# A planner inside the kernel sets the order on every engine; cache splits move to ACT and GpSimd

## The chip, the cores and the metric

The kernel runs on one core of a Trainium2 chip. A core has five engines with a queue each, worked off in order: PE (TensorE, matmuls), DVE (VectorE), ACT (ScalarE), POOL (GpSimd) and SP, which here only issues DMAs. Matmuls write PSUM, which DVE and ACT read; POOL works between SBUF tiles. The metric is the time of one execution on the device in microseconds (us); lower is better. Times are medians of a few runs, and one more execution is taken with the hardware profiler.

## The reference

The reference is one step of a two-layer hybrid encoder. It has 512 new prompt frames (called P below: four tiles of 128 rows) and 8 running streams with 16 new frames each (called S: one tile of 128 rows), and the streams have 1024 cached positions per layer.

```python
def trunk_layer(x, q_pos, past, ...):
    p = x @ w_in
    a_u, a_v, b_cq, b_ckv, b_kr, c_q, c_k, c_v = jnp.split(p, in_split_points(), axis=-1)
    y_a = spatial_gate(u, layer_norm(gelu(a_v)), w_s, b_s)
    # latent attention: scores against cached and new ckv and krope, softmax, values are ckv
    out_lat = sweep_query_blocks(lambda qp, ql, qr: mla_attend(qp, ql, qr, ckv_all, kr_all, k_pos),
                                 q_pos, q_lat, q_rope)
    # stick-breaking attention: log-sigmoid, suffix sum, exp, cached and new k and v
    y_c = sweep_query_blocks(lambda qp, qq: sb_attend(qp, qq, k_all, v_all, k_pos), q_pos, qc)
    y = jnp.concatenate([rms_norm(y_a, g_a), rms_norm(y_b, g_b), rms_norm(y_c, g_c)], -1)
    x = layer_norm(ALPHA * x + y @ w_out, ln1_g, ln1_b)
    h = jnp.square(jax.nn.relu(x @ w_up + b_up)) @ w_down + b_down
    return layer_norm(ALPHA * x + h, ln2_g, ln2_b), (ckv, krope, kc, vc, v)
```

Each layer runs for P (no past) and for S (with the cache). All numbers are float32.

## The kernel before

**Split products.** Each float32 operand is split into a high half, a rounding cast to fp32r (on ACT, `act.copy`), and a low half, the difference (`sub`, on DVE unless another engine is named). `mm3` then does three fp32r matmuls: high by high, high by low, low by high. So every weight tile and cache tile that is loaded costs a cast, a subtraction and its matmuls.

**Work per layer.** P projects all five row tiles at once (`in`, `mix`), and beside it does its stick-breaking attention and the gate. Then come P's latent attention (`lane_pmla`: tiles ckT, knT, krT, vM, qT, pT), its output projection, and the MLP in groups of four 128-wide slices (`w_up` in tile wx, `w_down` in tile w or w8, activations in hT). S is a second thread: `s_prep`, latent attention over the cache (`lane_smla`), stick-breaking attention over the cache (`lane_ssb`), output projection and MLP (tile wS). S takes its rows from P's projection of the same layer, and P's next layer takes S's row tile.

**The cache pieces of S.** Keys come as 128 x 512 pieces: DMA to rawK, ACT cast to cT, DVE subtraction to cT (`sample_scores`, L1106). In the latent attention every second key piece has a rope piece too, krs to kr, with the cast on ACT and the subtraction of the lower 64 partitions on DVE (L1201). Values come as 128 x 512 pieces: DMA to rawV, DVE cast to cN, POOL subtraction to cN (`sample_values`, L1143, L1144). Each of these tags has two buffers.

**What sets the order.** `weave` and `lanes` interleave the generators of P and S by a rough running clock for each engine (`Pace`, `cost_of`) and by shares of PE time (`RATE`). The program thus written then goes to the framework's own scheduler, which orders each engine's queue by its own estimates. The framework adds all waits on semaphores and the reuse of buffers; the order on an engine is fixed when the program is built. Nearly all instructions carry line L109, that of the recording helper, so groups go by tile names. In the trace, w8 reads w.

Of the kernel before, what the change touches and what calls it, by code (L numbers as in the profile page):

```python
# [44 lines left out]
FW = 3.0  # L45

# [5 lines left out]
class Pace:  # L52


    def __init__(self):
        self.free = dict(pe=0.0, act=0.0, dve=0.0, pool=0.0)
        self.done, self.read, self.slots = {}, {}, {}
        self.pe = self.t = 0.0

    def add(self, key, cost, out, ins):  # L60
        s = max([self.free[key]] + [self.done.get(x, 0.0) for x in (out, *ins)])
        self.t = self.free[key] = s + cost
        self.done[out] = self.t + 0.1
        for x in ins:
            self.read[x] = self.t + 0.1
# [17 lines left out]
def cost_of(key, name, out, ins):  # L83
    n = math.prod(out.shape[1:])
    if name == "transpose":
        return 0.109 if ins[0].dtype == F32 else 0.056
    if key == "pe":
        return max(n / 2400, math.prod(ins[0].shape[1:]) / 1200)
    if name in ("tensor_reduce", "bn_stats"):
        n = math.prod(ins[0].shape[1:])  # L90
    return {"act": 0.11 + n * 0.00072, "dve": 0.07 + n * (0.00052 if name == "tensor_copy" else 0.00104),
            "pool": 0.07 + n * 0.0023}[key]


class Timed:
# [5 lines left out]
    def __getattr__(self, name):  # L101
        f = getattr(self.eng, name)
        if name.startswith("preload"):
            return f

        def call(out, *a, **k):
            ins = [x for x in (*a, *k.values()) if isinstance(x, bass.AP)]
            self.pace.add(self.key, cost_of(self.key, name, out, ins), out.tensor.name, [x.tensor.name for x in ins])
            return f(out, *a, **k)  # L109
        return call  # L110

# [48 lines left out]
def hybrid_step(  # L160
# [9 lines left out]
    ld, pace = nc.sync, Pace()  # L170
# [4 lines left out]
    cp = ecx(tc.tile_pool(name="const", bufs=1))  # L175
    rawp = ecx(tc.tile_pool(name="raw", bufs=1))
    wp = ecx(tc.tile_pool(name="w8", bufs=4))
    xp = ecx(tc.tile_pool(name="xy", bufs=1))
    sm = ecx(tc.tile_pool(name="small", bufs=3))
    drp = ecx(tc.tile_pool(name="scr", bufs=1, space=DRAM))  # L180
    ps = ecx(tc.tile_pool(name="ps", bufs=1, space=PSUM))
# [11 lines left out]

    act.preload_act_table_set("natural_log_exp_and_others")
# [1338 lines left out]
```

## Time and profile before

| | us |
|---|---|
| median of 3 runs | 1856.31 (1853.24 to 1859.94) |
| the profiled execution | 1860.24 |
| its span, first to last instruction | 1858.5 |
| PE busy in the span | 1724.9 |
| DVE busy | 1307.1 |
| ACT busy | 931.0 |
| POOL busy | 342.6 |

Busy is the time in which an engine has at least one instruction running. A matmul's end is modelled and overlaps the next one's start, so PE's busy time is more than its work. [...] In the profile's rows, "out<-in" names the tile written and the tiles read, and what stands behind "<-" at the end of a row is what the instruction waited for.

### The profile page before, as it was taken

Reading aid. Unit: us, or ns where it says so; the run is one execution under the profiler, and the core shown is the slowest. Engines: PE = TensorE matmul, PEld = TensorE weight load, DVE = VectorE, ACT = ScalarE, POOL = GpSimd, SP = SyncE. Lnnn points to the kernel's source line nnn. Section 1 sums busy time; section 2 is a strip of 40 time slices with the busy share of each in tenths; the row PEclk is TensorE's granted clock in tenths of the full one; section 3 lists DMA queues with packets and bytes.
Section 4 is the critical chain, followed back from the end, with each engine's and each line's share of the span. In section 5 each row is a group of like instructions: output and inputs, shape, how many; then the busy total and the mean of one; then the engine's idle time right before and its main releaser. Section 6 shows DMA issues by size and latency. Waiting matters only on the chain. (4 is left out here: it accounts for less than half of the span.)

```text
span 1858.5 us, 24372 instructions
## 1 busy us (share of the span) xinstructions
PE 1724.9 (93%) x8756; PEld 1460.2 (79%) x8756; DVE 1307.1 (70%) x1870; ACT 931.0 (50%) x1613; POOL 342.6 (18%) x338
## 2 busy tenths in 40 slices
PE   8998897989999999999799988979899999999997
PEld 7887785878778888888688876858787778888886
DVE  3576978687885577676626768886878765776766
ACT  4674756245653346564227547661455623465641
POOL 0023123350213110001000321323502332000001
PEclk9998979989999999999899988889999999999999
DMA  7225654544544467784442245554445433776852
GB/s 260 89 79 156 185 180 143 177 128 141 183 136 130 135 243 253 215 265 149 133 157 83 75 155 179 182 164 147 140 136 170 147 113 104 259 240 215 268 162 90
DMA packets 145817, 305.05 MB, mean 164 GB/s; under 512 B 32032, under 2 KB 46496, under 8 KB 145696
## 3 DMA queue, kind: packets, MB, share of 16 engines
q1 hardware_dynamic: 145696, 303.49, 51.1%
q8 instruction: 69, 1.13, 0.3%
q14 instruction: 52, 0.43, 0.1%
HBM read 286.14 MB, written 17.30 MB: 163 GB/s over the span
## 5 line engine op out<-in xcount | busy, mean ns | idle before, releaser
L109 PE MATMUL acc<-w,hT 128*128 128x512 f32 x1536 | 399.5, 401 | 6.7 <-DVE xy L109 3.9
L109 PE MATMUL acc<-yT,wx 128*128 128x512 f32 (+1 forms) x1632 | 397.0, 388 | 6.7 <-ACT wx L109 3.2
L109 PEld LDWEIGHTS acc<-yT,wx 128*128 128x128 f32 x1632 | 298.4, 194 | 68.1 <-ACT wx L109 3.7
L109 PEld LDWEIGHTS acc<-w,hT 128*128 128x128 f32 x1536 | 288.7, 191 | 75.0 <-DVE xy L109 6.4
L109 POOL TENSOR_TENSOR cN<-rawV,cN 128x512 fp32r<-128x512 f32 x128 | 196.2, 1538 | 605.9 <-DVE cN L109 584.8
L109 DVE TENSOR_TENSOR w<-rawP,w 128x1024 fp32r<-128x1024 f32 (+4 forms) x122 | 147.9, 1213 | 135.7 <-ACT w L109 134.5
L109 DVE TENSOR_TENSOR wS<-rawS,wS 128x1024 fp32r<-128x1024 f32 x144 | 175.6, 1223 | 84.8 <-ACT wS L109 84.1
L109 ACT CAST wS<-rawS 128x1024 fp32r<-128x1024 f32 x144 | 151.0, 1052 | 128.3 <-PE sC L109 50.4
L109 ACT CAST w<-rawP 128x1024 fp32r<-128x1024 f32 (+4 forms) x122 | 122.4, 1006 | 179.4 <-DMA rawP<-in_w_down_dram 105.7
L109 PE MATMUL acc<-w,xT 128*128 128x512 f32 (+3 forms) x960 | 194.3, 355 | 0.0
L109 PEld LDWEIGHTS acc<-w,xT 128*128 128x128 f32 x960 | 161.8, 197 | 15.5 <-DVE ev L109 0.4
L109 DVE TENSOR_TENSOR xy<-xy,acc 128x512 f32<-128x512 f32 x128 | 85.8, 682 | 49.1 <-PE acc L109 48.4
L109 POOL TENSOR_SCALAR rs<-mv 128x1 f32<-128x1 f32 x20 | 14.2, 710 | 518.9 <-DVE mv L109 518.4
L109 ACT CAST cT<-rawK 128x512 fp32r<-128x512 f32 x128 | 78.7, 620 | 54.9 <-DMA rawK<-in_t_sbk_dram 17.8
L109 PE MATMUL x<-wS,htS 128*128 128x512 f32 x384 | 105.3, 394 | 0.0
L109 DVE TENSOR_TENSOR cT<-rawK,cT 128x512 fp32r<-128x512 f32 x128 | 93.7, 738 | 16.2 <-ACT cT L109 15.5
L109 PE MATMUL sC<-wS,x1TS 128*128 128x512 f32 x384 | 103.4, 393 | 0.0
L109 PE MATMUL x<-cN,pTs 128*128 128x256 f32 x512 | 91.1, 293 | 11.6 <-POOL cN L109 7.1
L109 PEld LDWEIGHTS x<-cN,pTs 128*128 128x128 f32 x512 | 78.9, 195 | 23.0 <-POOL cN L109 9.4
L109 DVE TENSOR_TENSOR wx<-rawP,wx 128x1024 fp32r<-128x1024 f32 x68 | 85.5, 1262 | 11.3 <-ACT wx L109 10.9
L109 DVE CAST cN<-rawV 128x512 fp32r<-128x512 f32 x128 | 73.2, 578 | 27.7 <-PE x L109 14.9
L109 PEld LDWEIGHTS sC<-wS,x1TS 128*128 128x128 f32 x384 | 72.0, 188 | 16.4
(278 smaller groups left out, 2808.1 us busy)
## 6 DMA issues: line engine op xcount, KB each, us to landing
rawP<-in_t_wup_dram SPq DMA_DIRECT2D x64, 512.0 KB, 4.0
rawP<-in_w_down_dram SPq DMA_DIRECT2D x64, 512.0 KB, 4.3
rawS<-in_w_up_dram SPq DMA_DIRECT2D x64, 512.0 KB, 4.5
rawS<-in_w_down_dram SPq DMA_DIRECT2D x64, 512.0 KB, 4.4
rawK<-in_t_ckv_dram SPq DMA_DIRECT2D x64, 256.0 KB, 3.2
rawV<-in_t_ckvv_dram SPq DMA_DIRECT2D x64, 256.0 KB, 3.0
rawK<-in_t_sbk_dram SPq DMA_DIRECT2D x64, 256.0 KB, 3.2
rawV<-in_t_sbv_dram SPq DMA_DIRECT2D x64, 256.0 KB, 2.9
```

The costliest lines, as they stand in the source:

```text
L109: return f(out, *a, **k)
```

## The change

Three parts. First, every instruction and DMA is noted when it is written (`Plan.note`), with its engine, a duration from a formula per engine and operation (`cost_of`), and its dependencies. Second, at the end a list schedule over the whole program is made (`Plan.schedule`): each engine, and SP for DMAs, takes at its next free moment the instruction with the lowest rank of those that are ready, and buffers and pools are granted in turn. The rank is the progress of a thread in its layer: P by its PE time, S by its time on other engines, with S laid between 0.25 and 0.93 of P's layer. `Plan.follow` then ties each engine's instructions to that order. Third, three kinds of work change engine: the cast of cached values goes from DVE to ACT (the subtraction stays on POOL), the subtractions of cached keys and of rope keys go from DVE to POOL. The matmuls are the same.

```diff
+SPAN = 0.25, 0.93
...
+class Plan:
+    AFTER = dict(pe=0.17, act=0.0, dve=0.0, pool=0.0, sp=0.0)
+    HOP = dict(pe=0.055, act=0.035, dve=0.035, pool=0.08, sp=0.03)
+    LAP = dict(pe=0.0, act=0.1, dve=0.08, pool=0.0, sp=0.0)
...
+    def ranks(self, lo, hi):
+        total, at = collections.Counter(), []
+        for o in self.ops:
+            key = o["by"], int(o["phase"][-1])
+            total[key] += o["cost"] if (o["eng"] == "pe") == (o["by"] == "P") and o["eng"] != "sp" else 0.0
+            at.append((key, total[key]))
+        at = [(c / max(total[k], 1e-9), k) for k, c in at]
+        at = [(k[1] + (f if k[0] == "P" else lo + (hi - lo) * f), i) for i, (f, k) in enumerate(at)]
...
+        def issue(k, e, s):
+            nonlocal dma
+            o = ops[k]
+            if o["kind"] == "copy":
+                s = max(s, free["pool"])
+            if e == "sp":
+                free[e] = s + 0.42
+                dma = max(dma, s + 1.3) + o["bytes"] / 320e3
+                f = dma + 0.45
+            else:
+                free[e] = s + o["cost"] - self.LAP[e]
+                f = s + o["cost"] + self.AFTER[e]
+                if o["kind"] == "copy":
+                    free["pool"] = max(free["pool"], f)
...
+    def follow(self, tc, order):
+        for e, ks in order.items():
+            for a, b in zip(ks, ks[1:]):
+                tc.add_manual_dep(self.ops[b]["ins"], self.ops[a]["ins"].name,
+                                  mybir.DependencyInfo(mybir.DependencyClass.NoSync, mybir.DependencyReason.DATA), reason="plan")
...
-def cost_of(key, name, out, ins):
+def cost_of(key, name, out, ins, accum):
     n = math.prod(out.shape[1:])
     if name == "transpose":
-        return 0.109 if ins[0].dtype == F32 else 0.056
+        return 0.1 if ins[0].dtype == F32 else 0.085
     if key == "pe":
-        return max(n / 2400, math.prod(ins[0].shape[1:]) / 1200)
+        return max(n * 0.000435 + 0.008, 0.111)
...
+    if key == "act":
+        return 0.19 + n * 0.00084 + 0.19 * accum + 0.06 * (len(ins) > 1)
+    if key == "dve":
+        if name == "scalar_tensor_tensor":
+            return 0.145 + n * 0.0013
+        slope = {"tensor_copy": 0.00054, "tensor_scalar": 0.0006, "tensor_tensor_scan": 0.0021}.get(name, 0.00107)
+        return 0.145 + n * slope
+    if name == "tensor_tensor":
+        return 0.55 if n <= 16 else 0.18 + n * 0.00218
...
+    VLO = KLO = pool
+    WLO = None
...
-                    split(c4[:, 0], c4[:, 1], raw)
+                    split(c4[:, 0], c4[:, 1], raw, KLO)
...
-                    dve.tensor_copy(v[:, 0], rv)
-                    sub(v[:, 1], rv, v[:, 0], pool)
+                    split(v[:, 0], v[:, 1], rv, VLO)
...
-                sub(kr[64:128], raw[64:128], kr[64:128])
+                sub(kr[64:128], raw[64:128], kr[64:128], pool)
...
     weave(nc, pace, thread(p_layer), thread(s_layer), RATE, now)
+    order = pace.plan.schedule(pace.plan.ranks(*SPAN))
+    pace.plan.follow(tc, order)
```

What this does to the queues is seen best in layer 0 where P's latent attention (knT, krT, qT, pT, vM, rawP on bank acc) and S's latent attention (cT, kr, cN on banks sC and x) meet. PE before, in the middle of that part:

```order
L109 MATMUL acc_2683<-vM_1792,pT_2444 128x256
L109 MATMUL acc_2683<-vM_1792,pT_2444 128x128
L109 MATMUL acc_2683<-vM_1792,pT_2444 128x256
L109 MATMUL acc_2683<-vM_1792,pT_2444 128x128
L109 MATMUL acc_2715<-identr_78,p_2520 128x128 x3
L109 MATMUL sC_2251<-cT_2177,qlT_1666 128x512 x2
L109 MATMUL sC_2251<-cT_2182,qlT_1666 128x512 x2
L109 MATMUL sC_2251<-kr_2187,qrS_1667 128x512
L109 MATMUL x_2245<-cN_2242,pTs_2190 128x256 x4
L109 MATMUL x_2245<-cN_2248,pTs_2190 128x256 x4
L109 MATMUL acc_2722<-vM_1792,pT_2672 128x256
L109 MATMUL acc_2722<-vM_1792,pT_2672 128x128
```

PE now, at the same point of P's work (the prompt's tile pairs with pT):

```order
L403 MATMUL acc_2578<-identr_78,rawP_2562 128x128 x3
L403 MATMUL sC_2041<-cT_2033,qlT_1666 128x512
L403 MATMUL sC_2041<-kr_2038,qrS_1667 128x512
L403 MATMUL sC_2104<-cT_2055,qlT_1666 128x512
L403 MATMUL acc_2600<-identr_78,rawP_2562 128x128 x3
L403 MATMUL sC_2104<-cT_2055,qlT_1666 128x512
L403 MATMUL acc_2606<-identr_78,p_2418 128x128 x3
L403 MATMUL acc_2621<-vM_1792,pT_2315 128x256
L403 MATMUL acc_2621<-vM_1792,pT_2315 128x128
L403 MATMUL acc_2621<-vM_1792,pT_2315 128x256
L403 MATMUL acc_2621<-vM_1792,pT_2315 128x128
L403 MATMUL acc_2664<-identr_78,p_2467 128x128 x3
```

Before, a key group (two cT tiles and kr) and two value tiles of S stand whole between two steps of P. Now P's steps follow each other more closely, with single matmuls of S between them, and S's value tiles come later.

DVE before, in the same part (cT, cN and kr are cache pieces of S, the rest attention work of P and S):

```order
L109 TENSOR_TENSOR pT_2672<-acc_2668,pT_2672 128x384
L109 SCALAR_TENSOR_TENSOR xy_80<-acc_2683,lr_2103,xy_80 128x128
L109 TENSOR_TENSOR cT_2256<-rawK_2254,cT_2256 128x512
L109 CAST cN_2310<-rawV_2308 128x512
L109 TENSOR_TENSOR cT_2267<-rawK_2265,cT_2267 128x512
L109 CAST cN_2319<-rawV_2317 128x512
L109 TENSOR_TENSOR s2_2174<-sC_2251,tmp_2262 64x512
L109 TENSOR_TENSOR kr_2352<-krs_2350,kr_2352 64x512
L109 TENSOR_TENSOR pT_2719<-acc_2715,pT_2719 128x384
L109 SCALAR_TENSOR_TENSOR xy_80<-acc_2722,lr_2486,xy_80 128x128
```

DVE now, in the same part:

```order
L403 TENSOR_TENSOR knT_2860<-acc_2862,knT_2860 128x2x256
L403 TENSOR_TENSOR vM_2861<-acc_2894,vM_2861 128x4x128
L403 TENSOR_TENSOR qT_3003<-acc_2984,qT_3003 128x512
L403 TENSOR_TENSOR cqT_3065<-acc_3082,cqT_3065 128x3x128
L403 TENSOR_TENSOR s2_1955<-sC_2166,tmp_2172 64x128
L403 TENSOR_TENSOR s2_1955<-s2_1955,mskm_1953 128x128
L403 TENSOR_TENSOR cqT_3065<-acc_3088,cqT_3065 128x3x128
L403 TENSOR_TENSOR ckT_3094<-acc_3106,ckT_3094 128x512
L403 TENSOR_REDUCE m_3132<-acc_3118 128x2
L403 TENSOR_TENSOR s2_1955<-sC_2163,tmp_2193 64x512
```

Between P's steps there stood two key subtractions, two value casts and a rope subtraction; none of these kinds is left on DVE.

POOL before, from the first cache piece of layer 0:

```order
L109 TENSOR_TENSOR cN_2242<-rawV_2240,cN_2242 128x512
L109 TENSOR_TENSOR cN_2248<-rawV_2246,cN_2248 128x512
L109 TENSOR_TENSOR cN_2310<-rawV_2308,cN_2310 128x512
L109 TENSOR_TENSOR cN_2319<-rawV_2317,cN_2319 128x512
L109 TENSOR_TENSOR cN_2361<-rawV_2359,cN_2361 128x512
L109 TENSOR_TENSOR cN_2384<-rawV_2382,cN_2384 128x512
```

POOL now, from the first cache piece of layer 0:

```order
L403 TENSOR_TENSOR cT_1958<-rawK_1956,cT_1958 128x512
L403 TENSOR_TENSOR cT_1963<-rawK_1961,cT_1963 128x512
L403 TENSOR_TENSOR kr_1968<-krs_1966,kr_1968 64x512
L403 TENSOR_TENSOR cT_1995<-rawK_1993,cT_1995 128x512
L403 TENSOR_TENSOR cN_2271<-rawV_2269,cN_2271 128x512
L403 TENSOR_TENSOR cT_2033<-rawK_2031,cT_2033 128x512
L403 TENSOR_TENSOR kr_2038<-krs_2036,kr_2038 64x512
L403 TENSOR_TENSOR cT_2055<-rawK_2053,cT_2055 128x512
L403 TENSOR_TENSOR cN_2277<-rawV_2275,cN_2277 128x512
L403 TENSOR_TENSOR cT_2096<-rawK_2094,cT_2096 128x512
L403 TENSOR_TENSOR kr_2101<-krs_2099,kr_2101 64x512
L403 TENSOR_TENSOR cT_2109<-rawK_2107,cT_2109 128x512
```

The value subtractions stood alone; now the key and rope subtractions stand among them in the order in which the pieces are used.

## Rows read from the trace of the kernel before

**Rows 1.** The page, its first line and its line of engines: busy, share, instructions.

```profile
span 1858.5 us, 24372 instructions
PE 1724.9 (93%) x8756; PEld 1460.2 (79%) x8756; DVE 1307.1 (70%) x1870; ACT 931.0 (50%) x1613; POOL 342.6 (18%) x338
```

**Rows 2.** Chain of waits, near its end: start us, length us, what, how many steps.

```profile
1808.40 25.33 PE acc L109 x109
```

**Rows 3.** Timeline of PE: start us, length us, what, shape, how many.

```profile
473.56 1.11 PE L109 MATMUL x<-cN,pTs 128*128 128x256 f32 x8
...
705.74 0.60 PE L109 MATMUL sC<-identr,hS 128*128 128x128 f32 x4
```

**Rows 4.** Table: stretch, length, PE, PEld, DVE, ACT, POOL busy, granted clock, DMA, GB/s.

```profile
91.00:196.00 105.00, 92.99 (x603) 88.72 (x603) 74.54 (x149) 63.11 (x142) 30.28 (x52) 0.92 0.43 132
196.00:321.00 125.00, 104.08 (x604) 91.18 (x603) 106.61 (x207) 82.34 (x179) 27.99 (x25) 0.86 0.53 165
321.00:634.00 313.00, 298.35 (x1456) 248.02 (x1455) 230.86 (x304) 133.40 (x212) 90.09 (x65) 0.96 0.46 144
634.00:876.00 242.00, 242.00 (x1077) 197.15 (x1076) 169.04 (x180) 133.36 (x180) 9.02 (x9) 1.00 0.69 222
1117.00:1246.00 129.00, 105.29 (x605) 90.59 (x604) 109.42 (x211) 82.43 (x176) 29.23 (x24) 0.87 0.53 167
1246.00:1565.00 319.00, 298.56 (x1464) 247.86 (x1463) 236.98 (x309) 135.78 (x219) 102.72 (x67) 0.96 0.45 141
```

**Rows 5.** Groups of PE by shape, 196 to 321: count, busy, mean ns, idle before.

```profile
L109 PE MATMUL sC<-cT,qlT 128*128 128x512 f32 x59 | 23.4, 477 | 4.3 <-ACT cT L109 4.2
...
L109 PE MATMUL acc<-krT,qrT 128*128 128x256 f32 x4 | 0.8, 282 | 0.0
```

**Rows 6.** Groups by shape, whole span: the work that moves.

```profile
L109 POOL TENSOR_TENSOR cN<-rawV,cN 128x512 fp32r<-128x512 f32 x128 | 196.2, 1538 | 605.9 <-DVE cN L109 584.8 <-DMA krs<-in_t_kr_dram 18.2 <-issue 1.5
L109 DVE TENSOR_TENSOR cT<-rawK,cT 128x512 fp32r<-128x512 f32 x128 | 93.7, 738 | 16.2 <-ACT cT L109 15.5
L109 ACT CAST cT<-rawK 128x512 fp32r<-128x512 f32 x128 | 78.7, 620 | 54.9 <-DMA rawK<-in_t_sbk_dram 17.8 <-DMA rawK<-in_t_ckv_dram 16.9 <-PE sC L109 14.3
L109 DVE CAST cN<-rawV 128x512 fp32r<-128x512 f32 x128 | 73.2, 578 | 27.7 <-PE x L109 14.9 <-DMA rawV<-in_t_ckvv_dram 5.2 <-DMA rawV<-in_t_sbv_dram 4.4
L109 DVE TENSOR_TENSOR kr<-krs,kr 64x512 fp32r<-64x512 f32 x32 | 25.9, 811 | 2.8 <-ACT kr L109 1.9
```

**Rows 7.** Timelines of POOL, then of DVE, 470 to 490.

```profile
471.23 2.01 POOL L109 TENSOR_TENSOR cN<-rawV,cN 128x512 fp32r<-128x512 f32 x1 [1.50 <-DVE cN L109]
478.08 1.30 POOL L109 TENSOR_TENSOR cN<-rawV,cN 128x512 fp32r<-128x512 f32 x1 [0.41 <-DVE cN L109]
...
478.12 1.81 DVE L109 TENSOR_TENSOR hT<-relu,hT 128x512 fp32r<-128x512 f32 x1
479.85 0.68 DVE L109 TENSOR_TENSOR cT<-rawK,cT 128x512 fp32r<-128x512 f32 x1
```

**Rows 8.** Stretches: cT (PE, PEld, DVE, ACT), cN (PE, PEld, DVE, POOL), kr (like cT).

```profile
196.00:321.00 125.00, 23.41 (x59) 11.64 (x59) 19.17 (x29) 17.07 (x28) 0.86 0.53 165
321.00:634.00 313.00, 22.69 (x64) 11.83 (x64) 21.96 (x32) 19.79 (x32) 0.96 0.46 144
...
196.00:321.00 125.00, 14.00 (x77) 11.46 (x77) 11.46 (x18) 25.50 (x18) 0.86 0.53 165
321.00:634.00 313.00, 32.55 (x181) 28.61 (x179) 23.83 (x44) 63.71 (x45) 0.96 0.46 144
...
196.00:321.00 125.00, 6.55 (x15) 3.11 (x15) 12.17 (x15) 9.26 (x15) 0.86 0.53 165
```

**Rows 9.** Timelines of PE, then of DVE, at the layer boundary.

```profile
927.54 2.82 PE L109 MATMUL acc<-identr,xy 128*128 128x128 f32 x12 [9.84 <-DVE xT L109]
...
918.05 1.28 DVE L109 SCALAR_TENSOR_TENSOR xy<-xy,rs,gl 128x1024 f32<-128x1024 f32 x1
```

**Rows 10.** The page, costliest groups: PE on the cached values.

```profile
L109 PE MATMUL x<-cN,pTs 128*128 128x256 f32 x512 | 91.1, 293 | 11.6 <-POOL cN L109 7.1
```

More of the change, by code (lines that the diff above doesn't have):

```diff
@@ L1 @@
+import collections
+import heapq
 import math
@@ L52 @@
 class Pace:
+    AFTER = dict(pe=0.22, act=0.06, dve=0.06, pool=0.1)
     def __init__(self):
[L56 removed]
+        self.free = dict(pe=0.0, act=0.0, dve=0.0, pool=0.0, sp=0.0, dma=0.0)
         self.done, self.read, self.slots = {}, {}, {}
         self.pe = self.t = 0.0
+        self.plan = Plan()
     def add(self, key, cost, out, ins):
@@ L62, in add, with load, new_slot @@
         self.t = self.free[key] = s + cost
-        self.done[out] = self.t + 0.1
+        self.done[out] = self.t + self.AFTER[key]
         for x in ins:
-            self.read[x] = self.t + 0.1
+            self.read[x] = self.t + self.AFTER[key]
         if key == "pe":
             self.pe += cost
-    def new_bank(self, tag, name, bufs):
+    def load(self, out, src, nbytes):
+        s = max(self.free["sp"], self.done.get(out, 0.0), self.done.get(src, 0.0))
+        self.free["sp"] = s + 0.1
+        self.free["dma"] = max(self.free["dma"], s + 1.7) + nbytes / 200e3
+        self.done[out] = self.read[src] = self.free["dma"] + 0.2
+    def new_slot(self, tag, name, bufs):
         names = self.slots.setdefault(tag, [])
@@ L72, in new_bank @@
         if len(names) > bufs:
-            self.done[name] = self.read.get(names[-1 - bufs], 0.0)
+            old = names[-1 - bufs]
+            self.done[name] = max(self.read.get(old, 0.0), self.done.get(old, 0.0))
     def bank(self, tag, bufs):
@@ L102, in __getattr__, with __init__, dma_start, tile @@
         f = getattr(self.eng, name)
-        if name.startswith("preload"):
-            return f
         def call(out, *a, **k):
-            ins = [x for x in (*a, *k.values()) if isinstance(x, bass.AP)]
-            self.pace.add(self.key, cost_of(self.key, name, out, ins), out.tensor.name, [x.tensor.name for x in ins])
-            return f(out, *a, **k)
-        return call
+            if name.startswith("preload"):
+                r = f(out)
+                self.pace.plan.note(self.key, 1.3, r.ins, [], [])
+                return r
+            ins = [x for n, x in [*enumerate(a), *k.items()] if isinstance(x, bass.AP) and n != "accum_out"]
+            outs = [out] + ([k["accum_out"]] if "accum_out" in k else [])
+            cost = cost_of(self.key, name, out, ins, "accum_out" in k)
+            self.pace.add(self.key, cost, out.tensor.name, [x.tensor.name for x in ins])
+            r = f(out, *a, **k)
+            kind = "copy" if self.key == "dve" and name == "tensor_copy" else ""
+            self.pace.plan.note(self.key, cost, r.ins, outs, ins, kind)
+            return r
+        return call
+class Loads:
+    def __init__(self, eng, pace):
+        self.eng, self.pace = eng, pace
+    def dma_start(self, out, src):
+        self.pace.load(out.tensor.name, src.tensor.name, 4 * math.prod(out.shape))
+        r = self.eng.dma_start(out, src)
+        self.pace.plan.note("sp", 0.42, r.ins, [out], [src], "", 4 * math.prod(out.shape))
+        return r
+class Slots:
+    def __init__(self, pool, pace, side=None, psum=False):
+        self.pool, self.pace = pool, pace
+        self.plan = pace.plan.new_pool(side, psum)
+    def tile(self, shape, dtype, tag=None, name=None, bufs=1):
+        t = self.pool.tile(shape, dtype, tag=tag or name, name=name, bufs=bufs)
+        self.pace.new_slot((id(self), tag or name), t.tensor.name, bufs)
+        self.pace.plan.new_tile(self.plan, tag or name, t.tensor.name, math.prod(shape[1:]) * (2 if dtype == BF16 else 4), bufs)
+        return t
 def lanes(pace, *gens):
@@ L173, in hybrid_step, with pool_in @@
     ecx = ctx.enter_context
[L175 to L181, printed above, removed]
+    def pool_in(**k):
+        return Slots(ecx(tc.tile_pool(bufs=1, **k)), pace, None if "space" in k else "left", k.get("space") == PSUM)
+    cp, rawp, wp, xp, sm = (pool_in(name=n) for n in ("const", "raw", "w8", "xy", "small"))
+    drp = pool_in(name="scr", space=DRAM)
+    ps = pool_in(name="ps", space=PSUM)
     ring = {"P": (rawp, RAW["P"])}
-    now = {"P": "in0", "S": "start0", "by": "P"}
+    now = pace.plan.now = {"P": "in0", "S": "start0", "by": "P"}
     def little(shape, dtype, tag):
@@ L1433, in hybrid_step @@
     weave(nc, pace, thread(p_layer), thread(s_layer), RATE, now)
+    order = pace.plan.schedule(pace.plan.ranks(*SPAN))
+    print("PLAN span", pace.plan.span, "pe idle", pace.plan.idle)
+    pace.plan.follow(tc, order)
 _INS = ["x_prompt", "x_sample", "cache_mla_ckv", "cache_mla_krope", "cache_sb_k", "cache_sb_v",
```

237 lines of the change are left out of this document (225 added, 12 removed).

## The prediction

> **What bounds the kernel now.** I read the page's first part, then the table of stretches, then the groups of the moved work. The page has PE busy for 93% of the span, DVE 70%, ACT 50%, POOL 18% [rows 1]. The 93% hides the loss, since the ends of matmuls are modelled, so I count PE's own work instead. In the chain of waits 109 matmuls of 512 columns in a row took 25.33 us, 0.232 each [rows 2]. Eight of 256 columns took 1.11 us, of which the last one's modelled 0.29 is more than its turn, so 0.117 each; four of 128 took 0.60, so 0.11 each [rows 3]. 384 and 320 columns are put in proportion (0.174, 0.145).
>
> The table of stretches [rows 4] shows where PE loses. From 634 to 876 it loses nothing: 1077 matmuls, nearly all of 512 columns, in 242 us. From 196 to 321 the prompt's latent attention (P) runs beside the streams' latent attention over the cache (S). Its 604 matmuls (27 groups, the first and the last in [rows 5]; 94 of 512 columns, 20 of 384, 237 of 256, 253 of 128) are 21.8 + 3.5 + 27.7 + 27.8 = 81 us of work in 125. DVE is busy for 106.6 of them, 85%, PE's granted clock is 0.86 on the mean, a part of it at the lower level, and DMA is at 0.53. So DVE is the limit there. The same count gives 81 of 129 for 1117 to 1246, the same part of layer 1; 283 of 313 and 283 of 319 for the two stretches behind them (output projection and the MLP while S's attention goes on); 81 of 105 for 91 to 196 (projections and stick-breaking), whose twin in layer 1 loses as much. Start, layer boundary and end hold some 33 us more. In all about 240 us of the span are not PE's work.
>
> **What moves between engines.** S splits each piece of cached keys or values into a high half (a cast) and a low half (a subtraction). DVE loses 128 key subtractions (93.7 us), 128 value casts (73.2) and 32 rope-key subtractions (25.9) [rows 6]: 193 us. ACT gets the value casts, 128 at the 620 ns of its cast of keys in the same shape [rows 6]: 79 us. POOL gets 128 key subtractions in the shape in which it already does the values, 1538 ns [rows 6]: 197 us, and 32 rope subtractions of 64 x 512, which the trace doesn't show on POOL. They can't be below nothing, since POOL did none of them; the nearest rows, of 128 x 512, are 1.30 and 2.01 [rows 7]; I take 1.4, near the lower as the tile is smaller: 45 us. POOL goes from 343 to 585 us, 31% of the span.
>
> From 196 to 321, DVE spends 19.2 us on key subtractions, 11.5 on value casts and 12.2 on rope keys [rows 8]: 42.8 go, and 106.6 becomes 64. ACT gets 18 casts, 11 us: 82.3 becomes 93.5. The move alone would make ACT the next limit there.
>
> **What moves in order.** On PE, between layer 0's first matmul on ckT and its last on vM (P's attention), the order had 64 matmuls on S's cT, 16 on kr, 64 on cN; now it has 28, 7 and 16 (layer 1: 28, 7, 19). By the prices above, with the small ones that go along, 31.9 us of S work becomes 11.9. So 20 us leave each attention stretch and enter the MLP stretch behind it. PE's work becomes 61 us. ACT's 93.5 lose 0.6 of the S casts (17.1 of keys, 9.3 of rope keys [rows 8], 11 of values): 22, and up to 10 for evictions and exponentials of the same pieces, so 61 to 71. DVE has at most 64. Elapsed time over the busiest engine is 125/106.6 = 1.17 now; kept, it gives 72 to 83, and I take 78, as three engines are then nearly level. The stretch gives back 125 - 78 - 20 = 27 us, its twin 31: **-58**.
>
> The MLP stretches take the 20 us in, so 303 us of PE work. In 321 to 634 DVE's 230.9 us lose 22.0 of keys and 23.8 of value casts [rows 8] and gain some 10: 195 of about 323, 60%. ACT goes from 133 to about 190. POOL has 26 us there without the cache, and gets the layer's 64 values, 64 keys and 16 rope keys less the 4, 14 and 7 tiles beside the attention: 182, so 208 of 323. From 634 to 876 DVE is at 70% and PE loses nothing [rows 4], so what is lost here is pieces that come late. Now 30 and 36 us are lost; the bounds are nothing and as much as now; I take 20 each, nearer to now, since POOL's share is new: **-26**.
>
> The mixed stretches have almost the same PE order and no cache work; between nothing and -16, I take **-4**. At the layer boundary PE waits 9.84 us for xT; one norm step of 1.28 us on DVE [rows 9] now stands ahead of the last MLP sum instead of behind it: **-1**. SP issues the same DMAs, in an order that differs by where S stands; start and end read alike: 0.
>
> New waits: on POOL the norm steps of P (a scale and a power) now stand behind subtractions of 1.3 to 2.0 us, and DVE's next scaling waits for them with other DVE work queued behind it. Matmuls of other row tiles hide that. Without this cover 70 such steps in the program at 1.5 us would be 105 us of DVE, half of what it was relieved of. I count none.
>
> Sum: -58 - 26 - 4 - 1 = -89, from the profiled execution's 1860.2 to 1771. That execution lies 0.2% above the median of the runs shown, 1856.3, so I forecast **1767 us**.
>
> [...] A POOL subtraction that came first took 1.30 us and one beside DVE work 2.01; a DVE subtraction that began 0.04 us after one on POOL took 1.81, one that met none 0.68 [rows 7]. [...] The rows speak for the move even so, as POOL is idle for 82%. [...]
>
> **Rivals.** (1) *The halves on POOL hold DVE.* The planner's price for them is 0.18 + 512 x 0.00218 = 1.30 us, the undisturbed one, and it lets only DVE's copies wait for POOL. If each of the 160 added ones holds a DVE instruction for half its length, 0.65 us, DVE gets 104 of the 193 us back, 54%; 46% of the gain is left, 41 us: 1819, 1815 against the median. For it: 1.81 and 2.01. Against it: most of DVE's attention work reads PSUM and showed no such hold.
>
> (2) *Slower: POOL's halves come late and PE stands.* 256 tiles are fed by POOL, and PE's order is fixed with their matmuls ahead of P's, in stretches that lose little now. If each comes x later than planned and PE stands for it, 256x is lost; the gain of 89 is gone at x = 0.35, and from 0.37 the kernel is slower. At x = 0.48, between the mean's 1.54 - 1.30 = 0.24 and the worst row's 0.71, it is 123 us: 1894, 1890 against the median. For it: POOL's mean is already 0.24 over its price. Against it: PE waits only 7.1 us for POOL's cN over 512 matmuls now [rows 10], and a late piece delays PE, so that the next is less late.
>
> (3) *No change: P's own chain is the limit.* If score, softmax, transpose and values follow each other too closely for any order, the attention stretches stay at 125 and 129 with 20 us less in each, so +40 - 26 - 5 = +9: 1869, 1865 against the median; without the MLP stretches' part anywhere from there to now. Against it: DVE's 85%.
>
> **Chances.** Forecast 0.62, with a range of its own from 1715 to 1805: 72 us in the attention stretches, no loss in the MLP ones and -16 in the mixed ones give 1703 against the median, 83 us and no gain in the MLP stretches 1803. Held DVE 0.24, late POOL 0.08, no change 0.06. About 0.3%, 5.6 us, is what a measurement here can tell. Faster by more than that: 0.62 + 0.24 and 0.01 of the last, 0.87; the same 0.04; slower 0.08 + 0.01. The range, 1715 to 1835, leaves out the late POOL, the last case and the far end of the forecast's own.
>
> **What would show it.** Right: from the first ckT to the last vM matmul near 80 us in each layer, DVE's total at 1110 to 1150, ACT's near 1010, POOL's 580 to 650, the MLP stretches losing 20 us each. POOL subtractions with a mean near 1.8 and DVE's w and hT subtractions well above 1.22 and 0.68 would show the first rival; PE idle before matmuls on cN and cT and put to POOL, tens of us in sum, the second; an attention stretch still over 115 us, the third. A time over 1835 makes the prediction wrong.

## The result, and the profile after

The changed kernel takes 1795.34 us, median of four runs (1792.59 to 1797.17), against 1856.14 for the kernel before: ratio 0.967, 95% interval 0.9648 to 0.9692. The forecast was 1767, so 61 us came of 89. The page of the profiled execution (1795.59 us), first line and engines:

```profile
span 1793.8 us, 24450 instructions
PE 1683.3 (94%) x8756; PEld 1408.1 (78%) x8756; DVE 1181.2 (66%) x1582; ACT 994.7 (55%) x1739; POOL 584.8 (33%) x498
```

Against [rows 1], POOL came out as worked out (585); ACT's 995 is 15 us under the forecast's 1010. DVE lost 126 us of busy time, though 193 us of work left it. The groups of the moved work, and two that stayed on DVE:

```profile
L403 POOL TENSOR_TENSOR cN<-rawV,cN 128x512 fp32r<-128x512 f32 x128 | 189.8, 1488 | 154.1 <-ACT cN L403 152.3 <-PE x L403 0.8
L403 POOL TENSOR_TENSOR cT<-rawK,cT 128x512 fp32r<-128x512 f32 x128 | 187.9, 1475 | 192.5 <-ACT cT L403 167.3 <-DMA rawK<-in_t_ckv_dram 22.4 <-PE acc L403 1.7
L403 DVE TENSOR_TENSOR wx<-rawP,wx 128x1024 fp32r<-128x1024 f32 x68 | 96.1, 1414 | 18.3 <-ACT wx L403 17.9 <-PE x L403 0.2
L403 ACT CAST cN<-rawV 128x512 fp32r<-128x512 f32 x128 | 78.8, 620 | 80.8 <-DMA rawV<-in_t_ckvv_dram 28.3 <-PE x L403 24.8 <-DMA rawV<-in_t_sbv_dram 18.3
L403 DVE TENSOR_TENSOR relu<-relu 128x512 f32<-128x512 f32 x64 | 57.4, 897 | 25.3 <-ACT relu L403 25.3
L403 POOL TENSOR_TENSOR kr<-krs,kr 64x512 fp32r<-64x512 f32 x32 | 45.6, 1425 | 28.4 <-ACT kr L403 23.9 <-PE acc L403 2.3 <-POOL cT L403 0.9
```

The same two DVE groups of the kernel before:

```profile
L109 DVE TENSOR_TENSOR wx<-rawP,wx 128x1024 fp32r<-128x1024 f32 x68 | 85.5, 1262 | 11.3 <-ACT wx L109 10.9
L109 DVE TENSOR_TENSOR relu<-relu 128x512 f32<-128x512 f32 x64 | 46.0, 718 | 10.0 <-ACT relu L109 10.0
```

The casts and the rope subtractions cost what was taken (0.62, and 1.43 against 1.4). The POOL subtractions are no shorter than before, though the mean of the values fell from 1538 to 1488 ns: one instruction of before took 9.06 us, and the median is 1.30 us in both kernels. The same DVE work, in such groups as wx and relu, became longer: over all groups with the same count in both kernels by 48 us. So the sum of DVE's durations fell by 147 us; its busy time fell by less because its instructions overlap each other less now (by 87 us before, 67 after).

To compare stretches, the bounds are put at the same work in both kernels: the prompt's attention runs from its first ckT matmul to its last vM matmul; the MLP stretch from there to the last matmul on cN (output projection and MLP beside S's attention). The granted clock is a share of full speed; the traces of both kernels have it at 1.00 (the upper level) or 0.50 (the lower), and a value between is a mean of the two. The table of stretches (length, PE, PEld, DVE, ACT, POOL busy, granted clock, DMA share, GB/s), of before for attention and MLP stretch of layer 0, the layer boundary, and both of layer 1:

```profile
178.00:316.80 138.80, 118.39 (x722) 104.92 (x721) 119.73 (x235) 91.96 (x201) 29.15 (x24) 0.88 0.56 173
316.80:629.60 312.80, 296.70 (x1455) 246.69 (x1455) 231.14 (x308) 134.64 (x216) 91.94 (x67) 0.96 0.45 144
914.90:1097.60 182.70, 159.89 (x938) 145.28 (x936) 103.83 (x178) 91.13 (x195) 30.94 (x58) 0.92 0.39 122
1097.60:1244.50 146.90, 122.77 (x742) 107.57 (x741) 119.81 (x234) 92.08 (x199) 29.23 (x24) 0.87 0.51 164
1244.50:1565.60 321.10, 300.29 (x1477) 249.36 (x1476) 237.86 (x312) 136.99 (x220) 102.72 (x67) 0.96 0.45 141
```

And after:

```profile
171.50:255.20 83.70, 78.91 (x586) 72.58 (x585) 64.04 (x134) 64.11 (x149) 37.14 (x32) 0.98 0.53 170
255.20:609.20 354.00, 327.67 (x1633) 266.09 (x1632) 227.12 (x269) 196.70 (x333) 204.19 (x140) 0.98 0.51 158
888.60:1060.60 172.00, 155.25 (x934) 140.77 (x932) 102.27 (x176) 90.88 (x195) 35.78 (x56) 0.96 0.41 127
1060.60:1148.10 87.50, 81.17 (x613) 74.37 (x612) 60.60 (x133) 65.03 (x152) 37.68 (x35) 1.00 0.49 156
1148.10:1503.10 355.00, 326.76 (x1627) 263.11 (x1627) 230.18 (x271) 197.64 (x335) 202.00 (x139) 0.98 0.51 160
```

PE's work in a stretch is its matmuls by shape times the prices of the forecast; the rest of the length is lost. For the attention of layer 0 after: 55 of 512 columns, 20 of 384, 245 of 256 and 263 of 128 are 12.8 + 3.5 + 28.7 + 28.9 = 73.8 of 83.7 us, 9.9 lost. So counted, both layers together: attention lost 94.1 and now loses 20.6 (-73.5); the MLP stretches lost 69.4 and now lose 90.5 (+21.1); all else, 77.5 and now 65.3 (-12.2). The sum, -64.7, is the difference of the spans.

What PE waits for in the MLP stretch of layer 1 after (us in total, times, longest), cut to S's pieces and sums:

```profile
PE sC L403 <- POOL cT L403: 3.7, 5, 1.3
PE x L403 <- ACT cN L403: 3.2, 3, 1.5
PE x L403 <- DVE z L403: 3.1, 1, 3.1
PE x L403 <- POOL cN L403: 2.8, 5, 0.9
PE sC L403 <- DVE o L403: 2.3, 3, 1.4
PE x L403 <- POOL cT L403: 1.1, 2, 0.9
PE sC L403 <- ACT cT L403: 1.0, 1, 1.0
PE x L403 <- ACT cT L403: 0.8, 1, 0.8
```

The rows on S's cached pieces and sums in the same stretch of before:

```profile
PE x L109 <- DVE cT L109: 2.2, 2, 1.9
PE sC L109 <- DVE o L109: 0.4, 1, 0.4
PE x L109 <- ACT cT L109: 0.2, 1, 0.2
```

There are many short waits on single pieces now. Taking each matmul that starts over 0.12 us later than its price allows, and what its last semaphore waited for, waits on halves of cached pieces are 8 us in the two MLP stretches of before and 28 us after.

### The profile page after: what moved, and what is told of

Same layout as the page of the kernel before. It is cut to its first block, busy times and chain, and to the rows that moved or that the text cites. A ratio compares the mean times of both kernels' runs of the same rounds, so it can differ in the third digit from the quotient of the medians.

```text
span 1793.8 us, 24450 instructions
## 1 busy us (share of the span) xinstructions
PE 1683.3 (94%) x8756; PEld 1408.1 (78%) x8756; DVE 1181.2 (66%) x1582; ACT 994.7 (55%) x1739; POOL 584.8 (33%) x498
## 4 chain that ended last, share of the span: by engine, by line
PE 56%; DVE 12%; DMA 10%; ACT 8%; POOL 7%; issue 6%; SPq 1%; POOLq 0%; ACTq 0%; DVEq 0%
PE acc L403 38%; PE sC L403 9%; PE x L403 8%; POOL rs L403 2%; POOL cN L403 2%; DVE xy L403 2%; DMA rawV<-in_t_ckvv_dram 2%; DVE a L403 2%; POOL cT L403 2%; DMA rawK<-in_t_ckv_dram 1%; DVE wx L403 1%; DMA rawP<-in_w_down_dram 1%; ACT w L403 1%; DVE z L403 1%; DVE w L403 1%
## 5 line engine op out<-in xcount | busy, mean ns | idle before, releaser
L403 PEld LDWEIGHTS acc<-yT,wx 128*128 128x128 f32 x1632 | 292.5, 191 | 59.7 <-DVE wx L403 1.7
L403 PEld LDWEIGHTS acc<-w,hT 128*128 128x128 f32 x1536 | 281.3, 188 | 66.5 <-ACT hT L403 6.0
L403 POOL TENSOR_TENSOR cT<-rawK,cT 128x512 fp32r<-128x512 f32 x128 | 187.9, 1475 | 192.5 <-ACT cT L403 167.3
L403 POOL TENSOR_TENSOR cN<-rawV,cN 128x512 fp32r<-128x512 f32 x128 | 189.8, 1488 | 154.1 <-ACT cN L403 152.3
L403 POOL TENSOR_SCALAR rs<-mv 128x1 f32<-128x1 f32 x20 | 22.1, 1105 | 522.9 <-DVE mv L403 521.8
L403 ACT CAST cN<-rawV 128x512 fp32r<-128x512 f32 x128 | 78.8, 620 | 80.8 <-DMA rawV<-in_t_ckvv_dram 28.3
L403 ACT CAST cT<-rawK 128x512 fp32r<-128x512 f32 x128 | 78.9, 619 | 56.7 <-DMA rawK<-in_t_ckv_dram 18.7
L403 DVE TENSOR_TENSOR wx<-rawP,wx 128x1024 fp32r<-128x1024 f32 x68 | 96.1, 1414 | 18.3 <-ACT wx L403 17.9
L403 PE MATMUL x<-cN,pTs 128*128 128x256 f32 x512 | 96.2, 294 | 12.5 <-POOL cN L403 6.9
L403 PE MATMUL x<-wS,htS 128*128 128x512 f32 x384 | 99.5, 394 | 0.5 <-DVE htS L403 0.4
L403 PEld LDWEIGHTS x<-wS,htS 128*128 128x128 f32 x384 | 71.9, 188 | 17.9 <-DVE htS L403 0.8
```

Source lines behind the costliest of these rows:

```text
L403: r = f(out, *a, **k)
```

## Experiments

The streams are S, the prompt P. Lost time is PE's, in us, both layers together; "clock" is the mean granted clock of the span; "lead" is the time from the end of a piece's low half (cT, cN; 256 pieces) to the matmul that reads it, as median in us, and the number of leads under 0.5 us.

| kernel | median us | ratio to before, 95% | lost: attention | MLP | all else | clock | lead | <0.5 |
|---|---|---|---|---|---|---|---|---|
| before | 1856.14 | 1 | 94.1 | 69.4 | 77.5 | 0.953 | 3.4 | 36 |
| the change | 1795.34 | 0.967 (0.9648 to 0.9692) | 20.6 | 90.5 | 65.3 | 0.984 | 1.0 | 105 |
| order alone | 1806.21 | 0.971 (0.9677 to 0.9742) | 27.6 | 87.8 | 66.8 | 0.980 | 0.5 | 121 |
| engines alone | 1805.07 | 0.9702 (0.9673 to 0.9731) | 51.7 | 46.6 | 87.0 | 0.973 | 2.5 | 36 |
| keys on DVE | 1844.89 | 0.993 (0.9903 to 0.9957) | 24.8 | 128.9 | 71.6 | 0.960 | 0.7 | 117 |
| POOL price 1.50 | 1807.19 | 0.9719 (0.9687 to 0.9752) | 24.3 | 89.2 | 71.8 | 0.982 | 1.2 | 70 |
| slack 0.5, all | 1792.15 | 0.9662 (0.9633 to 0.9692) | 20.5 | 85.2 | 69.4 | 0.984 | 0.9 | 90 |
| slack 1.0, S | 1806.88 | 0.9748 (0.9712 to 0.9783) | 24.0 | 90.7 | 70.1 | 0.978 | 1.7 | 50 |
| S until 1.0 | 1795.23 | 0.967 (0.9636 to 0.9704) | 19.6 | 82.3 | 70.5 | 0.979 | 1.7 | 72 |
| slack 3.0, pieces | 1795.13 | 0.9688 (0.9657 to 0.9719) | 29.7 | 77.4 | 70.9 | 0.976 | 3.4 | 3 |
| half plan | 1795.84 | 0.9699 (0.9667 to 0.9732) | 24.2 | 68.0 | 87.5 | 0.974 | 3.6 | 39 |
| half plan, old engines | 1816.73 | 0.9801 (0.977 to 0.9832) | 27.8 | 90.1 | 74.6 | 0.978 | 3.4 | 41 |
| middle free | 1852.41 | 0.997 (0.9949 to 0.999) | 24.8 | 135.8 | 76.3 | 0.953 | 3.1 | 63 |
| slack late | 1781.11 | 0.9581 (0.9544 to 0.9617) | 16.9 | 68.7 | 78.9 | 0.979 | 3.1 | 38 |

**The order alone, and the engines alone.**

```diff
-    VLO = KLO = pool
+    VLO, KLO = pool, None
...
-                    split(v[:, 0], v[:, 1], rv, VLO)
+                    dve.tensor_copy(v[:, 0], rv)
+                    sub(v[:, 1], rv, v[:, 0], pool)
...
-                sub(kr[64:128], raw[64:128], kr[64:128], pool)
+                sub(kr[64:128], raw[64:128], kr[64:128])
```

> The list schedule as in the change, but all three kinds of work on the engines of before (value casts, key and rope subtractions on DVE). PE's loss is its time less its work by shape; the changed kernel loses 10 and 11 us in the two attention stretches of the prompt (first ckT to last vM matmul) and 44 and 46 in the two stretches behind them (output projection and MLP beside the streams' attention), 176 in all. Theory A (the order gives the attention gain; late halves from POOL cost the MLP stretches): attention loses 13 each, MLP stretches about 33 each as before the change, some 1776 us. Rival B (DVE's relief gives the attention gain, not the order): attention loses 35 or more each, 1845 or above. Rival C (the streams' work in the MLP stretches is held by its own chain of scores, softmax and sums, not by POOL): attention 13, MLP stretches 45 each, some 1800.

The other one is the kernel before with these lines the other way round.

> The kernel before with the three kinds of work moved to ACT and POOL and the order left to the framework's scheduler; the order still has 29 us of the streams' work in each attention stretch. Theory A: attention loses about 30 each instead of 44 and 50, the MLP stretches about 8 each more than before: some 1838 us. Rival B: most of the gain is there without the list schedule, 1800 to 1810. If POOL's halves hold DVE as much as they relieve it: 1856, no change.

Attention and MLP stretch of layer 0, order alone:

```profile
173.60:261.10 87.50, 81.97 (x600) 75.25 (x600) 74.75 (x163) 62.97 (x145) 10.82 (x12) 0.97 0.51 163
261.10:606.30 345.20, 320.19 (x1580) 257.90 (x1579) 265.76 (x379) 160.04 (x268) 121.79 (x80) 0.97 0.50 159
```

The same, engines alone:

```profile
184.70:298.50 113.80, 98.75 (x697) 88.18 (x697) 75.69 (x157) 92.35 (x204) 83.62 (x66) 0.98 0.65 201
298.50:611.80 313.30, 297.31 (x1493) 246.07 (x1493) 206.18 (x241) 165.42 (x274) 152.87 (x106) 0.99 0.47 148
```

The order alone came out as rival C had it: attention loses 27.6, but the MLP stretches 87.8 with the old engines too, so the move to POOL is not the cause; waits on halves are 41 us in them, 17 on POOL's, 17 on DVE's, 7 on ACT's. Theory A falls in that, and rival B with it. In the attention stretch of layer 0 DVE is busy for 74.8 of 87.5 us, 85%, and was for 119.7 of 138.8, 86%: its share is as before, so the order shortens the stretch by taking DVE's work out of it too, and DVE may still set its length. The engines alone took the time of rival B, 1805: 42 us less lost in attention, though 29 us of S's work stay in each of those stretches, and 23 us less in the MLP stretches, close to the 26 forecast for them. ACT is the busiest beside PE in attention then, 92.4 of 113.8 us, as the forecast said of the move alone. The two halves of the change bring 0.029 and 0.030 apart and 0.033 together; the intervals overlap. They cure the same stretch, and the order undoes what the engines gain in the other.

**Keys back on DVE, and another price for POOL.**

```diff
-    VLO = KLO = pool
+    VLO, KLO = pool, None
...
-                sub(kr[64:128], raw[64:128], kr[64:128], pool)
+                sub(kr[64:128], raw[64:128], kr[64:128])
```

> The changed kernel with the key and rope subtractions back on DVE (planned so); only the value casts are moved, to ACT, and POOL does the value subtractions as before. Theory A (late halves from POOL cost the MLP stretches): POOL has 340 us instead of 585, the MLP stretches lose about 35 each instead of 45, attention about 12 each, some 1778 us. Rival C (the streams' own chain): MLP stretches 45 each, 1798. If DVE's relief by the keys is what counts: attention over 20 each and 1815 or more.

```diff
-        return 0.55 if n <= 16 else 0.18 + n * 0.00218
+        return 0.55 if n <= 16 else 0.18 + n * 0.00258
```

> The changed kernel, the planner's price for a POOL subtraction of 512 columns raised from 1.30 to 1.50 us, near the 1.48 that it took. Only the order changes. Theory A: PE's waits on cT and cN in the MLP stretches halve, they lose about 35 each, some 1776 us. Rival C, or lateness that no price can mend: 1790 to 1800.

Neither did all that a theory said. Keys on DVE took a time of the last theory, 1815 or more, but not by its way, over 20 lost in each attention stretch: attention loses 25 in both layers together, the MLP stretch of layer 1 39, but that of layer 0 90. A stretch of it, and PE's largest group in the same stretch:

```profile
295.00:374.00 79.00, 51.93 (x173) 39.45 (x174) 28.52 (x50) 34.09 (x67) 24.87 (x22) 0.50 0.43 119
```

```profile
L403 PE MATMUL x<-cN,pTs 128*128 128x256 f32 x71 | 23.4, 465 | 11.7 <-POOL cN L403 6.7 <-ACT cN L403 4.3 <-DVE pTs L403 0.7
```

PE has almost only S's matmuls there, stands before many of them, and the granted clock is 0.50 for all of it; the other engines are idle for most of it. What brought S alone on PE is ACT's order. The prompt's output projection needs the norm of all its rows, and the sum of squares of the last row tile (junk on ACT) stands in ACT's queue behind S's whole latent attention. DVE's last sum for this tile, and that instruction, in this kernel:

```profile
265.80 0.34 DVE L403 SCALAR_TENSOR_TENSOR xy<-acc,lr,xy 128x128 f32<-128x128 f32 x1
```

```profile
366.15 0.63 ACT L403 ACTIVATE junk<-xy 128x512 bf16<-128x512 f32 x1
```

And in the change:

```profile
255.90 0.35 DVE L403 SCALAR_TENSOR_TENSOR xy<-acc,lr,xy 128x128 f32<-128x128 f32 x1
```

```profile
256.38 0.63 ACT L403 ACTIVATE junk<-xy 128x512 bf16<-128x512 f32 x1
```

So the step came 100 us after its input here and 0.1 us in the change, and the output projection's first matmul at 373 instead of 266. Why the plan set it there is open. The price nearer to the measured one changed the MLP loss by 1 us (44 and 45, as rival C had it, at a time 7 us over its range): its cause is no wrong price for POOL.

**Slack in the plan.**

```diff
-                hop = 0.0 if ops[x]["eng"] == e == "pe" else f + self.HOP[ops[x]["eng"]]
+                hop = 0.0 if ops[x]["eng"] == e == "pe" else f + self.HOP[ops[x]["eng"]] + (0.5 if ops[x]["eng"] == "pe" else 0.0)
```

> The changed kernel, with the planner made to start a matmul 0.5 us later than before after an instruction of another engine that it waits for; only the order changes. In the four kernels traced so far, the list schedules put PE's matmul within 0.5 us behind the end of the low half that it reads for 105 and 121 of 256 pieces, the framework's order for 36 and 36, and the list schedules lose 44 to 46 us in each MLP stretch of layer 0, the framework's 26 to 33. Theory D (the list schedule leaves PE no slack behind the pieces, so each small delay stands on PE): within 0.5 us falls under 50 of 256, the MLP stretches lose about 30 each, attention up to 14 each: some 1770 to 1778 us. Rival C (the streams' own chain sets the pace there, and a planned slack only moves it): 44 each still, 1790 to 1805. Rival E (the slack makes P's chains longer): attention over 18 each, 1810 or more.

The next adds 1.0 and only where `ops[x]["by"] == "S"`.

> The same with 1.0 us, and only for the streams' matmuls (by S); the prompt's are planned as in the change. Theory D: MLP stretches lose 25 to 30 each, attention 10 each as in the change, some 1762 to 1770 us. Rival C: 44 each, 1790 to 1800.

The third leaves the plan's times and sets `SPAN = 0.25, 1.0`.

> The changed kernel with the streams' work laid between 0.25 and 1.0 of the prompt's layer instead of 0.25 to 0.93, so the same pieces are spread over more of the MLP. Theory D: a piece is still read right when it is ready, so the loss of the two MLP stretches in sum stays within 10 of the change's 90: 1785 to 1800 us. Rival C: with more time for the streams' chain the loss falls by a quarter or more: 1770 or less.

The MLP loss is 85, 91 and 82 us, against 90 in the change; leads under 0.5 us fall from 105 to 90, 50 and 72. The first is no test of theory D, since its leads hardly changed. The second has half as many short leads, but loses as much, as rival C had it, and is 12 us slower than the change (intervals apart). The third came out as theory D had it, though its MLP stretches hold 60 us more work. Slack of 0.5 or 1.0 us brings little, and neither does laying S later by itself. So 3.0 us, about the middle lead of the kernel before, on the pieces alone (tiles cT, cN, kr):

> The changed kernel with 3.0 us of slack planned between a cached piece's halves and PE's matmuls on them, no other slack; the middle lead of the framework's order was 2.5 to 3.4 us, that of the change 1.0. With 1.0 us for all matmuls of the streams, waits on the halves still made some 18 us in the two MLP stretches, against 28 in the change. Theory D (lateness of the halves against the plan, larger than 1 us): waits on the halves fall under 8 us, MLP stretches 33 each, some 1770 us. Rival C (what is not waited for there is waited for behind it, in the streams' chain): the halves' waits fall but the stretches still lose 42 or more each, 1790 to 1805.

Theory D holds for the halves: 3 of 256 leads are under 0.5 us, waits on halves are 0.7 us in the MLP stretches, which lose 13 us less. Rival C had the time right, but not the place: in the MLP stretches waits for P's norm steps (xy, yT) rose by 10 us and those for the MLP's own pieces (hT, wx) by 6, while those for S's sums (o, z) stayed at 13 and 14; attention lost 9 us more, and all else 6 more.

**Order left to the framework in part.**

```diff
+        cut = [(first["out0"], first["in1"]), (first["out1"], 1e9)]
+        for e, ks in order.items():
+            last, open_ = None, []
+            for k in ks:
+                if any(x <= self.ops[k]["at"] < y for x, y in cut):
+                    open_.append(k)
+                    if last is not None:
+                        tie(k, last)
+                else:
+                    for x in open_ or ([last] if last is not None else []):
+                        tie(k, x)
+                    last, open_ = k, []
```

> The changed kernel, tied to the list schedule only from a layer's start to the end of the prompt's latent attention; from there to the layer's end (output projection, MLP) the framework orders each engine. The prompt's attention keeps 13 to 14 us of the streams' work instead of 29. Theory F (the list schedule's order itself costs in the MLP stretches, the framework's leaves more room): attention loses 10 to 13 each as in the change, the MLP stretches 21 to 28 each as with the engines alone, some 1755 to 1765 us. Rival C (20 us more of the streams' work in these stretches is what costs, whoever orders it): MLP stretches 42 or more each, 1790 to 1800.

> The same with value casts, key and rope subtractions on DVE as before the change. If DVE's relief is worth in the MLP stretches what the engines alone showed there (33 and 37 to 26 and 21): 12 us each more than in the kernel beside it, attention 2 to 5 each more, some 1785 us. If the moves bring nothing once the order is set: the same time as the kernel beside it.

The MLP stretches lose 68 instead of 90 although they hold more work (S's last cN matmul is 62 us later). That is the direction of theory F, which had 42 to 56, at over 30 us more than its time. But the framework puts P ahead, and S's own MLP ends behind P's; the last stretch of the half plan, from P's last matmul on hT to the end:

```profile
1753.30:1797.10 43.80, 30.41 (x123) 22.49 (x121) 31.60 (x33) 21.87 (x29) 4.39 (x4) 0.89 0.64 215
```

44 us with 27 us of work, so 17 lost against 9 in the change; this and the layer boundary (39 lost against 25) take the gain back. Beside it the old engines are 21 us slower (0.9801 against 0.9699, intervals apart). In the profiled executions, which lie 13 us apart, the MLP stretches lose 22 us more, attention 4 more and all else 13 less. So with these stretches left to the framework the moves pay.

The last two try to keep both. The first frees only the time from P's first `out` matmul to S's first `out` matmul:

```diff
-        cut = [(first["out0"], first["in1"]), (first["out1"], 1e9)]
+        cut = [(first[f"Pout{l}"], first[f"Sout{l}"]) for l in (0, 1)]
```

> The changed kernel, with the framework ordering only the stretch from the prompt's output projection to the first matmul of the streams' output projection; before and behind it the list schedule holds, so that the streams can't end late as they did when the whole rest of the layer was left to the framework (layer boundary 39 us lost and 27 us of work behind the prompt's last matmul). Theory F (the list schedule's order costs in that stretch): MLP stretches lose 30 to 36 each, the rest as in the change, some 1770 us. Rival C (the streams' 20 us more work there costs, whoever orders it): 42 or more each, 1790 to 1800.

All theories missed it by 52 us or more. The end of the freed stretch in layer 0, then PE's timeline in it (start, length, what, how many, idle before):

```profile
613.30:650.80 37.50, 25.25 (x83) 18.71 (x82) 4.11 (x9) 13.45 (x31) 15.94 (x14) 0.50 0.34 92
```

```profile
614.71 0.58 PE L420 MATMUL x<-cN,pTs 128*128 128x256 f32 x1 [1.02 <-ACT cN L420]
616.05 1.22 PE L420 MATMUL x<-cN,pTs 128*128 128x256 f32 x4 [0.76 <-POOL cN L420]
617.62 1.01 PE L420 MATMUL x<-cN,pTs 128*128 128x256 f32 x3 [0.34 <-POOL cN L420]
619.38 0.58 PE L420 MATMUL x<-cN,pTs 128*128 128x256 f32 x1 [0.75 <-ACT cN L420]
```

P's matmuls of the stretch are all done, S's last value pieces come one by one through cast, POOL and PE, and the clock stays at 0.50; in layer 1 the 48 us from 1524 to 1572 look alike, at a granted clock of 0.51. This is the forecast's second rival as it would look.

The second plans 3.0 us only for S's stick-breaking pieces and lets S reach to the layer's end:

```diff
-SPAN = 0.25, 0.93
+SPAN = 0.25, 1.0
...
+ (3.0 if ops[x]["eng"] == "pe" and ops[x]["phase"][:3] == "ssb" and any(t[:2] in ("cT", "cN") and t[2] == "_" for t in o["tiles"]) else 0.0)
```

> The changed kernel with 3.0 us of planned slack behind the halves only for the streams' stick-breaking attention, which lies wholly in the MLP stretches, and the streams laid between 0.25 and 1.0 of the prompt's layer. Theory D (waits on the halves are the removable part): 3.0 us for all pieces took 13 us from the MLP stretches and gave 13 back in the start and the prompt's attention; this one leaves these alone, so 1780 to 1786 us. If the waits only change their name: 1790 to 1800.

1781.11 us, faster than the change (0.9581 against 0.967, intervals apart). It came out as theory D had it. `SPAN` alone gave 0.967 and 1795.23 us (intervals apart), so with this `SPAN` the slack brings 14 us; it was not run without it. The MLP stretches of both layers:

```profile
258.20:642.90 384.70, 365.15 (x1801) 298.48 (x1800) 243.27 (x291) 205.82 (x345) 197.57 (x139) 0.98 0.48 154
1145.90:1527.90 382.00, 359.92 (x1800) 296.13 (x1800) 244.06 (x291) 209.83 (x350) 207.30 (x142) 0.99 0.49 157
```

They lose 35 and 34 us, 22 less than in the change with 80 us more work in them, and waits on halves are 14 us instead of 28. With `SPAN` alone they are 23, and the loss is 82, so 14 of the 22 us go with the slack. Attention kept its gain; all else lost 14 more, most of it at the layer boundary (34 against 25). S's last matmul on wS in layer 0 is now 5 us ahead of P's last on hT, in the change 47 us; but with `SPAN` alone it is 5 us too, and the boundary loses 27, so this doesn't explain it. A third buffer for each kind of piece was not tried.

## Why the prediction was right, and which term of it was not

Direction and range held; 1795 lies in the forecast's own range, 28 us over the 1767 forecast. By the terms:

- **Attention stretches, -58:** -73.5. Right in cause (S's work leaves, DVE is no longer the limit: 64 of 84 us), too small in size. The 1.17 of elapsed time over the busiest engine was carried over, which left 17 us lost per stretch; there are 10. PE's own work, 74 of the 84 us in layer 0, is now ahead of DVE's and ACT's 64 each, and PE's clock is 0.98 and 1.00 instead of 0.88 and 0.87.
- **MLP stretches, -26:** +21. This is the step that failed: "I take 20 each, nearer to now, since POOL's share is new"; 44 and 46 were lost. For the engines alone it came out near (-23, losing 26 and 21). It was wrong for the order: the list schedule puts PE's matmul behind its piece with a median lead of 1.0 us instead of 3.4, and waits on halves rose by 20 us, as the loss did by 21. The pieces' share is shown by the slack late: against the same `SPAN` without slack its stretches lose 14 us less. The lead is not the whole cause, and the rest stays open: 3.0 us for all pieces took away nearly all waits on halves and only 13 us of loss; and the half plan with the old engines has a median lead of 3.4 and 41 short ones, about as before, and still loses 90. There DVE is busy for 75% of the stretch of layer 0, with the moves (half plan, 68 lost) for 62%.
- **Mixed stretches and boundary, -5:** about -16 (start -5, boundary -10; the rest of all else is the MLP behind S's attention, +5, and the end, -1). Of it PE's wait for xT is -1.8; its row now, against [rows 9]:

```profile
898.51 2.82 PE L403 MATMUL acc<-identr,xy 128*128 128x128 f32 x12 [8.07 <-DVE xT L403]
```

  The rest was forecast near its small end; kernels planned nearly alike lose 65 to 72 in all else, so some of it goes with small changes of the order or from run to run.
- **Rivals.** (1) DVE is held, by 48 us instead of 104, in groups that read SBUF (wx, relu), while a large group that reads PSUM kept its length (xy<-xy,acc, 682 and 683 ns). The trace of after shows it instruction by instruction: 45 of relu that overlap no subtraction on POOL take 686 ns on the mean, 19 that overlap one 1397; for xy<-xy,acc it is 683 and 684. In the attention stretches DVE has idle time to hide it, 20 of 84 us in layer 0. DVE's total of 1181 is over the 1110 to 1150 given as a sign. The other sign was badly chosen: w and hT "well above 1.22 and 0.68" were at 1.28 and 0.84 before the change too, on the mean. (2) Late halves came true in small: 28 us of waits over 220 pieces, 0.13 us each, below the 0.35 from which they decide; but with the old engines they are 41 us, 17 of them on POOL's value halves, so the order makes them, not the moves to POOL. POOL's mean of 1.54, read as 0.24 over its price, hides that the median is 1.30, the price itself: some long ones, one of 9.06 us, make the difference. (3) P's chain is not the limit: the stretches fell to 84 and 88 us.
- **The slower engine.** A subtraction of 128 x 512 took 1.48 us on POOL after and 0.74 on DVE before [rows 6]. The kernel that leaves those of the keys on DVE, with the casts on ACT, is slower by 50 us, but 45 of these are lost in the MLP stretch of layer 0, with its 79 us at the lower clock and P's late norm step, so it proves little; in the attention stretches it loses 4 more. In the half plan, where old and new engines stand side by side, the three moves together bring 21 us.

**The clock,** which no term named, carries much of the gain. By 2 x (1 - clock) x span, since the lower level is 0.50, PE was at the lower level for 175 us before and 57 after. Before, a piece of such time and a run of equal matmuls in it, then one at the upper level:

```profile
233.80:247.50 13.70, 12.83 (x55) 12.35 (x56) 9.75 (x19) 5.74 (x10) 3.46 (x3) 0.50 0.68 215
```

```profile
244.99 2.67 PE L109 MATMUL acc<-ckT,w 128*128 128x256 f32 x12
...
248.32 1.03 PE L109 MATMUL acc<-vM,pT 128*128 128x256 f32 x8
```

From start to start that is 0.21 us each against 0.11. Matmul by matmul, what those at the lower level took beyond their price, up to twice the price, is 67 us before and 21 after: 46 of the 65 us. No run has it apart from the standing: of the stretches of before shown, the clock was lowest where PE stood most, 0.88 and 0.87 in attention with PE busy for 85% and 84%, and within them it was at 0.50 for the 13.7 us above with PE busy for 12.8, right behind 3.5 us in which PE was busy for 1.8. The MLP stretches show the other side: they lose more now, in many short waits, at a clock of 0.98 instead of 0.96.

## What to carry to other kernels

Two cures of one bound need not add (here 0.029 and 0.030 alone, 0.033 together): count each alone on the stretch it works in, and ask of each what it does in the stretch behind. An order made by a list schedule with measured durations closes the gaps of its plan, but places each consumer right behind its producer; plan a lead for pieces that pass three engines (here 3 us), and try it stretch by stretch, since given to all pieces it cost outside the MLP stretches what it brought in them. Where a fixed order makes a kernel much slower, look for an instruction of one thread that stands in a queue behind a whole stage of the other: one of 0.6 us kept P's output projection off PE for some 100 us. Look at the granted clock beside TensorE's idle time: in these kernels it was low where the idle time was dense (0.50 over 79 us with PE busy for 52; 0.98 over 355 with PE busy for 327).

## What the runs showed of the hardware that was not expected

- The lower clock, 0.50, lasted 79 us in the kernel with keys on DVE and 37.5 in the one with the middle free, with PE busy for 52 and 25 us of them and nearly only S's matmuls on it. In both, PE stood for a third of the time, in many short waits.
- A POOL subtraction of 64 x 512 takes 1.43 us on the mean and one of 128 x 512 takes 1.48 (medians 1.29 and 1.30): here half the partitions saved next to nothing.
- DVE's work from SBUF became longer beside POOL's greater load (relu 718 to 897 ns, wx 1262 to 1414). In the three other kernels with the subtractions of keys on DVE, relu is 752 to 790 and wx 1296 to 1301, so a part of relu's rise is the order's. The group that reads PSUM, xy<-xy,acc, stayed at 682 to 685 ns in all fourteen kernels.
